# Transposes on two row halves of TensorE, and one tile for four, in a fused decoder layer

## The chip, the cores and the metric

One core of a Trainium2 chip runs the whole kernel. The metric is the device time of one execution in microseconds, the median over several runs. TensorE (PE) multiplies, ScalarE (ACT) copies and casts and evaluates functions, VectorE (DVE) does elementwise work, GpSimd (POOL) small elementwise work and some DMA issues, SyncE (SP) issues most DMAs. Each engine takes its instructions in the order of its own queue and waits by semaphores for the others.

## The reference

```python
# x (1, 512, 1024) float32, D_FF = 2816
x = x + 0.5 * rms_norm(swiglu_ffn(rms_norm(x, g0), ffn1_w_in, ffn1_w_out), p0)
x = x + rms_norm(token_mixer(rms_norm(x, g1), w_mix_in, ..., w_mix_out), p1)
x = x + 0.5 * rms_norm(swiglu_ffn(rms_norm(x, g2), ffn2_w_in, ffn2_w_out), p2)

def swiglu_ffn(x, w_in, w_out):
    gate, up = split(x @ w_in, 2)
    return (silu(gate) * up) @ w_out
# token_mixer: h @ w_in, then 4 heads of a gated linear recurrence (HGRN2) and 4 heads of a
# stabilised mLSTM, each normalised and gated, side by side (y, 512 x 1024), then y @ w_mix_out
```

## The kernel before, in words

The 512 tokens are four token tiles of 128 (i = 0 to 3). Every float32 product is made of three matmuls of a high and a low part: `mm3` (L198 to L200, and the like at L549, L560, L619, L1004, L1012) multiplies high by high, high by low and low by high. The high part of an operand is a cast by ACT, the low part is what DVE gets when it subtracts the high part from the operand.

Products contract over the model dimension, so activations are transposed first. A transpose of a 128x128 block is a matmul with the block as stationary operand and the identity as moving operand; it lands in PSUM. `turn` (L364) puts four of them, the four k-tiles of one half h of the 1024 columns of a token tile, into one PSUM bank, and then ACT casts the bank of 512 columns into the high part in `xq` and DVE subtracts into the low part. Where the place is: `to_t` and `two` (L370, L371) at the boundary of FFN 1 and mixer and for y, `part` (L384, L386, and a plain copy to `xf` at L388) at the heads of the two FFNs for the token tiles 0 and 1. For tiles 2 and 3 `sums` makes combinations out of the same kind of transposes, because the FFNs' first products are done with a Strassen-like scheme over sums of halves (`xf` holds what the sums need).

`xq` is four SBUF tiles, one for each half of the tokens and half h of the model dimension; each holds the high and the low part (b) of four k-tiles of 256 tokens. Tile 0 has 16 columns more for each part, which `xh[0]` uses at the FFNs' heads:

```python
xq = {n: self.cp.tile([P, 2 * D + 2 * STEP * (n == 0)], F32R, name=f"xq{n}") for n in (1, 2, 3, 0)}
```

Other transposes: `ek` (L1403, two groups of six, copied to `kdt`), `qk` (L1672, six, whose results DVE multiplies into `kw`); the latter follow directly on L1632, matmuls of the mLSTM's scores which already run on the two row halves of the array.

The order of the work is that in which the program issues it; a scheduler of the framework places instructions in each engine's queue by priority and by what they read and write, and it sets the waits between the engines by the address ranges of the accesses to a tile. Weights are cast and subtracted beside the products (L294 and L296; with a row factor L299 and L302) into a pool `w`.

The places in order of time: boundary of FFN 1 and mixer (331 to 349 us), `ek` (405 and 449), `qk` (485), the first half of y (536, into `mix_out0`), the second half of y (549 to 559), the head of FFN 2 (579 and 582), where the residual stream and the normed input (`xn` or `hf`, L481) of each token tile are made one after the other: ACT squares and sums (L453), POOL takes the power (L458), DVE multiplies (L481), PE transposes, ACT casts, DVE subtracts.

Of the kernel before, what the change touches and what calls it, by code (L numbers as in the profile page):

```python
# [8 lines left out]
F32 = mybir.dt.float32  # L9
# [5 lines left out]
P = 128  # L15
# [108 lines left out]
class Layer:  # L124
    def __init__(self, ctx, tc, aps):
        self.tc, self.nc = tc, tc.nc
        self.__dict__.update(aps)
        nc = self.nc
        pool = lambda name, **kw: ctx.enter_context(tc.tile_pool(name=name, bufs=1, **kw))
        self.cp, self.wp, self.sp, self.psp = pool("cp"), pool("wp"), pool("sp"), pool("psp", space=PSUM)  # L130
        self.uid, self.hold = 0, ()
        self.wt, self.free, self.slot = None, deque(), {}

        self.ident = self.cp.tile([P, P], F32, name="ident")
        make_identity(nc, self.ident)
        self.nhalf = self.cp.tile([P, 8], F32, name="nhalf")
        nc.gpsimd.memset(self.nhalf, -0.5)
        self.xs = self.cp.tile([P, NT, D], F32, name="xs")

        xq = {n: self.cp.tile([P, 2 * D + 2 * STEP * (n == 0)], F32R, name=f"xq{n}") for n in (1, 2, 3, 0)}  # L140
        self.xt = [xq[n] for n in range(4)]
        self.xq = [t[:, : 2 * D].rearrange("p (b k t) -> p b k t", b=2, k=KH) for t in self.xt]

        x0 = self.xt[0].rearrange("p (b x) -> p b x", b=2)[:, :, :D].rearrange("p b (k t) -> p b k t", k=KH)
        self.xh = [x0, *self.xq[1:]]
        self.prm = self.cp.tile([P, 36], F32, name="prm")
        self.dram = dram = ctx.enter_context(tc.tile_pool(name="sums", bufs=1, space=bass.MemoryType.DRAM))
        self.sums_of = {
            (f, h, k2): dram.tile([P, 4, QUARTER], F32, name=f"{f}sums{h}_{k2}")
            for f in ("f1", "f2") for h in range(2) for k2 in OUT[f][h] if k2 in QUARTERED[f][h]  # L150
        }
# [212 lines left out]
            self.nc.tensor.transpose(pt[:, c * P : (c + 1) * P], src[:, k * P : (k + 1) * P], self.ident)  # L364
        return pt.rearrange("p (c t) -> p c t", c=4)

    def two(self, dst, i, src):

        v = slice((i % 2) * P, (i % 2 + 1) * P)
        self.nc.scalar.copy(dst[:, 0, :, v], src)  # L370
        self.low = self.nc.vector.tensor_tensor(dst[:, 1, :, v], src, dst[:, 0, :, v].bitcast(F32), op=ALU.subtract)  # L371

    def to_t(self, i, src, halves=(0, 1)):

        for h in halves:
            self.two(self.xq[2 * (i // 2) + h], i, self.turn(src, h))

    def part(self, i, h, src):

        pv = self.turn(src, h)  # L380
        v = slice(i * P, (i + 1) * P)
        dst = self.xh[h][:, :, :, v]
        yield
        self.nc.scalar.copy(dst[:, 0], pv)  # L384
        yield
        self.nc.vector.tensor_tensor(dst[:, 1], pv, dst[:, 0].bitcast(F32), op=ALU.subtract)  # L386
        yield
        self.nc.scalar.copy(self.xf[h][:, :, v], pv)  # L388
        yield

    def sums(self, i, src):
# [37 lines left out]
    def to_s(self, i, src):  # L429

        if i < 2:
            for h in range(2):
                g = self.part(i, h, src)
                for _ in range(3):
                    next(g)
                self.copies.append(g)
        else:
            self.gs.append(self.sums(i, src))
            next(self.gs[-1])
# [955 lines left out]
    def hgrn_edges(self, p, d):  # L1395

        nc = self.nc
        qd = self.qd[:, 2 * p : 2 * p + 2, :]
        nc.vector.tensor_tensor(qd, self.q[p][:, :, P:], qd, op=ALU.mult)
        for a in range(2):  # L1400
            pt = self.ps()
            for c in range(NT - 1):
                nc.tensor.transpose(pt[:, c * P : (c + 1) * P], d[:, a, c * P : (c + 1) * P], self.ident)  # L1403
            nc.scalar.copy(self.kdt[:, 2 * p + a, :], pt[:, : 3 * P])

    def hgrn_level(self, p, n, ke):

# [229 lines left out]
    def mlstm_scores(self, mc):  # L1637

        nc = self.nc
        self.mend = mc.tile([P, NH, NT], F32, name="mend")  # L1640
        self.pT = mc.tile([P, NH, T], F32, name="pT")
        w = mc.tile([P, NT, NH], F32, name="w")
        self.qdm = mc.tile([P, 2, 3 * P], F32, name="qdm")
        H = [self.mlstm_head(h) for h in range(NH)]

        next(H[0])
        next(H[1])
        for h in range(0, NH, 2):
# [20 lines left out]
        turned = [self.ps() for _ in range(2)]  # L1669
        for p, pt in enumerate(turned):  # L1670
            for c in range(3):
                nc.tensor.transpose(pt[:, c * P : (c + 1) * P], self.qk[:, 2 + p, c * P : (c + 1) * P], self.ident)  # L1672
        for p in range(2):
            wp = self.col(8)[:, :6]
            nc.vector.tensor_copy(wp.rearrange("p (c a) -> p c a", a=2), w[:, :3, 2 * p : 2 * p + 2])
            nc.vector.tensor_tensor(
                self.kw[:, p].rearrange("p c (a d) -> p (c a) d", a=2),
                turned[p][:, : 3 * P].rearrange("p (n d) -> p n d", d=64),
                wp[:, :, None].broadcast_to([P, 6, 64]),
                op=ALU.mult,  # L1680
            )
# [96 lines left out]
    def mixer(self):  # L1778
# [3 lines left out]
        with tc.tile_pool(name="ma", bufs=1) as ma:  # L1782
# [35 lines left out]
            with tc.tile_pool(name="mc", bufs=1) as mc:  # L1818
# [8 lines left out]
                self.until("hg")  # L1827
                self.chunks(self.hgrn_values, FILL[3])
                self.until("mo")
                for i in range(NT):  # L1830
                    self.to_t(i, self.y[:, i], (0,))
                self.mix_out0()

    def values_mv(self, ma, i, ps):
# [12 lines left out]
    def mix_out0(self):  # L1847
# [130 lines left out]
```

## Time and profile before

| | |
|---|---|
| median of 3 runs | 916.1 us (916.0 to 916.24) |
| the profiled execution | 916.13 us, span 914.4 us, mean granted clock 0.999 |
| PE busy | 906.1 us, 99% of the span, 7330 instructions |
| DVE, ACT, POOL busy | 84%, 57%, 20% |
| costliest groups on PE | L619 237.4 + 178.0 us, L1012 80.9, L1004 79.2 |
| transposes of L364 | 128 in all, 0.14 us for a weight load's record, 0.27 for a matmul's |

Records of matmuls overlap: an instruction's duration on PE holds the time until its result is out, and the next one starts while it runs. The rate is read from the distance between starts, or from a merged row's length less that of one, over their number less one.

### The profile page before, as it was taken

To read this page: it belongs to the slowest core of one execution; us is meant where nothing else is said; L and a number is where in the kernel's file an instruction comes from. 1 tells how busy PE (TensorE), PEld (TensorE's weight loads), DVE (VectorE), ACT (ScalarE), POOL (GpSimd) and SP (SyncE) were. 2 spreads that over 40 slices of the span, in tenths; PEclk is the share of its full clock that TensorE was granted. 3 is DMA by queue.
4 is the path that set the end of the run, shared out by engine and by line. 5 is a ranking of instruction groups with operands and counts; after the bars stand their busy time and mean duration, and the time that the engine had idled before them with its cause. 6 is when DMAs were issued, how large, how long until landed. Compare 5 with 4: busy or idle time off the path is not lost.

```text
span 914.4 us, 18150 instructions
## 1 busy us (share of the span) xinstructions
PE 906.1 (99%) x7330; PEld 874.9 (96%) x7330; DVE 767.2 (84%) x1005; ACT 522.0 (57%) x749; POOL 183.7 (20%) x256
## 2 busy tenths in 40 slices
PE   9999999999999999999999999999999999999997
PEld 8999999999999999998888887899999999999997
DVE  6899988889888876799896556799999889998886
ACT  7645545557566567957643345684454545757661
POOL 2541112121111047742230300322000000010002
PEclk9999999999999999999999999999999999999999
DMA  9355779775897815898953126253344445378542
GB/s 306 88 165 136 189 188 216 187 159 138 219 280 233 258 55 144 162 192 207 214 112 109 47 70 213 65 161 102 97 148 139 138 123 159 104 231 246 170 146 93
DMA packets 127921, 146.51 MB, mean 160 GB/s; under 512 B 16335, under 2 KB 100303, under 8 KB 127837
## 3 DMA queue, kind: packets, MB, share of 16 engines
q1 hardware_dynamic: 111868, 130.14, 46.4%
q0 software_dynamic: 15680, 14.69, 11.9%
q8 instruction: 57, 0.93, 0.4%
q10 hardware_dynamic: 288, 0.52, 0.2%
q14 instruction: 28, 0.22, 0.1%
HBM read 143.20 MB, written 31.48 MB: 191 GB/s over the span
## 4 chain that ended last, share of the span: by engine, by line
PE 62%; ACT 0%; DVE 0%; DVEq 0%; POOLq 0%; issue 0%; POOL 0%; ACTq 0%
PE ps L619 23%; PE ps L1012 8%; PE ps L549 6%; PE ps L198 5%; PE ps L200 5%; PE ps L199 5%; PE ps L1004 4%; PE ps L560 1%; PE ps L1441 1%; PE ps L364 1%; PE ps L1540 0%; PE ps L1742 0%; PE ps L1491 0%; PE ps L1715 0%; PE ps L1739 0%; PE ps L1717 0%
## 5 line engine op out<-in xcount | busy, mean ns | idle before, releaser
L294 ACT CAST w<-raw 128x1024 fp32r<-128x1024 f32 x246 | 250.6, 1027 | 192.0 <-PE ps L619 91.1
L296 DVE TENSOR_TENSOR w<-raw,w 128x1024 fp32r<-128x1024 f32 x246 | 299.4, 1221 | 30.3 <-ACT w L294 28.9
L619 PE MATMUL ps<-xq,w 128*128 128x256 f32 x2016 | 237.4, 277 | 0.0
L619 PEld LDWEIGHTS ps<-xq,w 128*128 128x128 f32 x2016 | 233.3, 188 | 0.1
L619 PE MATMUL ps<-sq,w 128*128 128x256 f32 x1512 | 178.0, 276 | 0.0
L619 PEld LDWEIGHTS ps<-sq,w 128*128 128x128 f32 x1512 | 174.6, 188 | 0.0
L310 DVE TENSOR_TENSOR raw<-raw,raw 128x1024 f32<-128x1024 f32 x72 | 89.7, 1252 | 7.5 <-DMA raw<-in_ffn_w_in_dram 6.2
L1012 PE MATMUL ps<-w,hs 128*128 128x256 f32 x672 | 80.9, 276 | 0.0
L1004 PE MATMUL ps<-w,hs 128*128 128x256 f32 x672 | 79.2, 276 | 0.0
L1012 PEld LDWEIGHTS ps<-w,hs 128*128 128x128 f32 x672 | 78.3, 188 | 0.0
L1004 PEld LDWEIGHTS ps<-w,hs 128*128 128x128 f32 x672 | 77.5, 188 | 0.0
L198 PE MATMUL ps<-w,xq 128*128 128x512 f32 x176 | 71.1, 405 | 0.1
L199 PE MATMUL ps<-w,xq 128*128 128x512 f32 x176 | 68.6, 391 | 0.0
L200 PE MATMUL ps<-w,xq 128*128 128x512 f32 x176 | 68.6, 391 | 0.0
L549 PE MATMUL ps<-xq,w 128*128 128x256 f32 x480 | 55.7, 277 | 0.0
L944 POOL DMA_DIRECT2D f2sums<-in_ffn_w_out_dram x15 | 20.0, 1507 | 177.5 <-DMA f2sums<-in_ffn_w_out_dram 177.0
L549 PEld LDWEIGHTS ps<-xq,w 128*128 128x128 f32 x480 | 54.9, 188 | 0.5 <-issue 0.5
L884 ACT CAST hs<-hf 128x1024 fp32r<-128x1024 f32 x32 | 33.7, 1054 | 28.0 <-PE ps L1012 20.3
L885 DVE TENSOR_TENSOR hs<-hf,hs 128x1024 fp32r<-128x1024 f32 x32 | 39.1, 1223 | 9.0 <-ACT hs L884 8.4
L944 POOL DMA_DIRECT2D f1sums<-f1sums x26 | 22.3, 859 | 110.1 <-DMA f1sums<-in_ffn_w_out_dram 56.1
L944 POOL DMA_DIRECT2D f2sums<-f2sums x30 | 26.3, 905 | 87.1 <-DMA f2sums<-in_ffn_w_out_dram 42.4
L310 POOL TENSOR_TENSOR raw<-raw,raw 128x1024 f32<-128x1024 f32 x12 | 32.6, 2724 | 40.9 <-DVE w L296 40.7
(263 smaller groups left out, 1232.9 us busy)
## 6 DMA issues: line engine op xcount, KB each, us to landing
raw<-in_ffn_w_in_dram SPq DMA_DIRECT2D x98, 512.0 KB, 4.7
raw<-in_ffn_w_out_dram SPq DMA_DIRECT2D x44, 512.0 KB, 5.1
raw<-in_w_mix_in_dram SPq DMA_DIRECT2D x28, 512.0 KB, 5.7
raw<-f2sums SPq DMA_DIRECT2D x15, 512.0 KB, 5.2
raw<-f1sums SPq DMA_DIRECT2D x13, 512.0 KB, 7.0
raw<-in_w_mix_out_dram SPq DMA_DIRECT2D x8, 512.0 KB, 4.3
f2sums<-in_ffn_w_out_dram SPq DMA_DIRECT2D x30, 128.0 KB, 5.0
f2sums<-in_ffn_w_out_dram SPq DMA_DIRECT2D x15, 256.0 KB, 6.1
```

Source lines behind the costliest of these rows:

```text
L198: mm(ps, sh, mh, start=start, stop=False, **kw)
L199: mm(ps, sh, ml, start=False, stop=False, **kw)
L200: mm(ps, sl, mh, start=False, stop=stop, **kw)
L294: nc.scalar.copy(hi, raw)
L296: self.low = nc.vector.tensor_tensor(lo, raw, hi.bitcast(F32), op=ALU.subtract)
L310: added = (nc.vector if late else nc.gpsimd).tensor_tensor(o, o, c, op=ALU.add)
L549: mm(ps[:, u0:u1], w[:, a, k, :], self.xop(k, b, u0, u1), start=k + n + m == 0, stop=k == ND - 1 and n == 2, skip_group_check=True,)
L619: self.nc.tensor.matmul(ps[:, c], wb[b][:, k, v], left[d][:, k, :], start=first and a + n + k == 0, stop=n == 2 and k == KH - 1, skip_grou ...
L885: self.nc.vector.tensor_tensor(lo, src, hi.bitcast(F32), op=ALU.subtract)
L944: nc.gpsimd.dma_start(to[:, a:b], v, accum_op=ALU.add)
L1004: mm(out, a[kk][:, i * P : (i + 1) * P], w[:, b, kk, QUARTER * v : QUARTER * (v + 1)], start=begin and c == kk == n == 0, stop=kk == 1 and ...
L1012: mm(ps[:, QUARTER * c : QUARTER * (c + 1)], A[a][:, c], B[b], start=begin and c == n == 0, stop=n == 2, skip_group_check=True,)
```

## The change

98 transposes are done as two transposes of 64 rows each, on the two row halves of the array. `turns` takes a list of up to eight blocks; for each it issues one transpose of the tokens 0 to 63 into the first of two PSUM banks, and one of the tokens 64 to 127 into the second. A bank so holds one half of the tokens of a tile (or of two tiles, `to_t2`) for eight blocks, 512 columns. A cast or a subtraction takes one bank, as before, but its result now goes to both halves h (or both token tiles), by an access pattern made with `pair`. The four `xq` tiles become one, since such a pattern must lie in one tile. The second half of y is transposed two token tiles at a time. The 32 transposes at the start of FFN 1 and the 16 in `sums` of FFN 2 stay as they are.

```diff
-        xq = {n: self.cp.tile([P, 2 * D + 2 * STEP * (n == 0)], F32R, name=f"xq{n}") for n in (1, 2, 3, 0)}
-        self.xt = [xq[n] for n in range(4)]
+        xq = self.cp.tile([P, 8 * D + 2 * STEP], F32R, name="xq")
+        self.xt = [xq[:, 2 * D * o : 2 * D * (o + 1) + 2 * STEP * (o == 3)] for o in (3, 0, 1, 2)]
...
+    def turns(self, srcs):
+        pts = [self.ps() for _ in range(2)]
+        for n, src in enumerate(srcs):
+            for u, pt in enumerate(pts):
+                r = slice(64 * u, 64 * u + 64)
+                self.nc.tensor.transpose(pt[:, 64 * n : 64 * n + 64], src[r], self.ident[r, r])
+        return [pt[:, : 64 * len(srcs)] for pt in pts]
...
+    def pair(self, a, b):
+        return bass.AP(a.tensor, a.offset, [a.ap[0], [b.offset - a.offset, 2], *a.ap[1:]])
...
+    def to_t(self, i, src):
+        x = self.xq[2 * (i // 2) : 2 * (i // 2) + 2]
+        for u, pt in enumerate(self.turns(self.tiles(src, ND))):
+            hi, lo = (self.pair(*(t[:, b, :, self.at(i, u)] for t in x)) for b in range(2))
+            self.parts(hi, lo, pt.rearrange("p (h k t) -> p h k t", h=2, t=64))
...
+    def part2(self, i, u, pt):
+        pv = pt.rearrange("p (h k t) -> p h k t", h=2, t=64)
+        v = self.at(i, u)
+        hi, lo = (self.pair(*(self.xh[h][:, b, :, v] for h in range(2))) for b in range(2))
+        self.nc.scalar.copy(hi, pv)
+        self.nc.vector.tensor_tensor(lo, pv, hi.bitcast(F32), op=ALU.subtract)
+        yield
+        self.nc.scalar.copy(self.pair(*(x[:, :, v] for x in self.xf)), pv)
         yield
...
         if i < 2:
-            for h in range(2):
-                g = self.part(i, h, src)
-                for _ in range(3):
-                    next(g)
+            for u, pt in enumerate(self.turns(self.tiles(src, ND))):
+                g = self.part2(i, u, pt)
+                next(g)
                 self.copies.append(g)
...
-                for i in range(NT):
-                    self.to_t(i, self.y[:, i], (0,))
+                for i in (0, 2):
+                    self.to_t2(i, 0, [self.y[:, i + n, :W] for n in range(2)])
...
-                if part:
-                    self.to_t(i, self.y[:, i], (1,))
+                if part and i % 2 == 0:
+                    self.to_t2(i, 1, [self.y[:, i + n, W:] for n in range(2)])
```

The places of `ek` and `qk` are changed in the same way (two calls of `turns` with six blocks each, and one with six). Lines move down: L364 splits into L364 (`turn`) and L373 (`turns`), L370 and L371 become L384 and L385, L384 and L386 of `part` become L423 and L424 of `part2`, L453 L490, L481 L518, L619 L656.

How it moves instructions: three places. The rows below are the engines' queues, in order; `xq_78`, `xq_75` and so on are the four tiles, `ps_...` PSUM banks, and the brackets name the engines that a row waits for.

ACT's queue at the head of FFN 2, where `xn` of tile 0 and `hf` of tile 1 have been transposed, before:

```order
443 L384 CAST xq_78<-ps_6607 128x4x128 [waits PE_49]
444 L384 CAST xq_75<-ps_6614 128x4x128 [waits PE_49]
445 L453 ACTIVATE junk_6594,col_6592<-xs 128x512 [waits DVE_49,Activation_49]
446 L453 ACTIVATE junk_6599,col_6597<-xs 128x512 [waits DVE_49,Activation_49,Pool_49]
447 L384 CAST xq_78<-ps_6633 128x4x128 [waits PE_49]
448 L384 CAST xq_75<-ps_6640 128x4x128 [waits PE_49]
449 L453 ACTIVATE junk_6661,col_6659<-ps_6434 128x512 [waits PE_49,Activation_49,Pool_49]
```

and after:

```order
443 L423 CAST xq<-ps_6686 128x2x4x64 [waits PE_49]
444 L490 ACTIVATE junk_6673,col_6671<-xs 128x512 [waits DVE_49,Activation_49]
445 L490 ACTIVATE junk_6678,col_6676<-xs 128x512 [waits DVE_49,Activation_49,Pool_49]
446 L423 CAST xq<-ps_6687 128x2x4x64 [waits DVE_49,PE_49]
447 L423 CAST xq<-ps_6720 128x2x4x64 [waits DVE_49,PE_49]
448 L423 CAST xq<-ps_6721 128x2x4x64 [waits DVE_49,PE_49]
449 L490 ACTIVATE junk_6756,col_6754<-ps_6513 128x512 [waits PE_49,Activation_49,Pool_49]
```

One cast moves behind the two squares, and three of the four casts wait for DVE besides PE.

DVE's queue at the same place, before:

```order
635 L386 TENSOR_TENSOR xq_78<-ps_6607,xq_78 128x4x128 [waits Activation_49]
636 L386 TENSOR_TENSOR xq_75<-ps_6614,xq_75 128x4x128 [waits Activation_49]
637 L481 SCALAR_TENSOR_TENSOR xn_6604<-xs,col_6602,gpre_6493 128x512 [waits DVE_49,Pool_49]
638 L481 SCALAR_TENSOR_TENSOR xn_6604<-xs,col_6602,gpre_6493 128x512 [waits DVE_49]
639 L386 TENSOR_TENSOR xq_78<-ps_6633,xq_78 128x4x128 [waits Activation_49]
640 L386 TENSOR_TENSOR xq_75<-ps_6640,xq_75 128x4x128 [waits Activation_49]
```

and after:

```order
635 L424 TENSOR_TENSOR xq<-ps_6686,xq 128x2x4x64 [waits Activation_49]
636 L518 SCALAR_TENSOR_TENSOR xn_6683<-xs,col_6681,gpre_6572 128x512 [waits DVE_49,PE_49,Pool_49]
637 L518 SCALAR_TENSOR_TENSOR xn_6683<-xs,col_6681,gpre_6572 128x512 [waits DVE_49]
638 L424 TENSOR_TENSOR xq<-ps_6687,xq 128x2x4x64 [waits Activation_49]
639 L424 TENSOR_TENSOR xq<-ps_6720,xq 128x2x4x64 [waits Activation_49]
640 L424 TENSOR_TENSOR xq<-ps_6721,xq 128x2x4x64 [waits Activation_49]
```

The second subtraction for tile 0 moves behind the two products that make `xn` of tile 2.

ACT's queue at the first half of y, where `mo` is the gate of the mLSTM's output and `w` a weight of `mix_out0`, before:

```order
411 L299 ACTIVATE w<-raw_6087,prm 128x512 [waits DMAHW7_49,PE_49]
412 L1843 ACTIVATE mo_6217<-ps_6007 128x512 [waits PE_49,Pool_49]
413 L370 CAST xq_78<-ps_6220 128x4x128 [waits PE_49]
414 L370 CAST xq_78<-ps_6227 128x4x128 [waits PE_49]
415 L370 CAST xq_76<-ps_6234 128x4x128 [waits PE_49]
416 L370 CAST xq_76<-ps_6241 128x4x128 [waits PE_49]
417 L299 ACTIVATE w<-raw_6087,prm 128x512
```

and after:

```order
411 L299 ACTIVATE w<-raw_6134,prm 128x512 [waits DMAHW7_49,PE_49]
412 L1877 ACTIVATE mo_6264<-ps_6054 128x512 [waits PE_49,Pool_49]
413 L299 ACTIVATE w<-raw_6134,prm 128x512
414 L384 CAST xq<-ps_6267 128x2x4x64 [waits PE_49]
415 L384 CAST xq<-ps_6268 128x2x4x64 [waits PE_49]
416 L384 CAST xq<-ps_6289 128x2x4x64 [waits PE_49]
417 L384 CAST xq<-ps_6290 128x2x4x64 [waits PE_49]
```

The second half of that weight moves ahead of the casts; the first two casts hold the tokens of tiles 0 and 1 together, the next two those of tiles 2 and 3.

More of the change, by code (lines that the diff above doesn't have):

```diff
@@ L365, in turn, with tiles, parts, at @@
         return pt.rearrange("p (c t) -> p c t", c=4)
[L367 to L376, printed above, removed]
+    def turns(self, srcs):
[5 more added lines that the diff above has]
+        return [pt[:, : 64 * len(srcs)] for pt in pts]
+    def tiles(self, src, n=4):
+        return [src[:, k * P : (k + 1) * P] for k in range(n)]
+    def pair(self, a, b):
+        return bass.AP(a.tensor, a.offset, [a.ap[0], [b.offset - a.offset, 2], *a.ap[1:]])
+    def parts(self, hi, lo, src):
+        self.nc.scalar.copy(hi, src)
+        self.low = self.nc.vector.tensor_tensor(lo, src, hi.bitcast(F32), op=ALU.subtract)
+    def at(self, i, u):
+        return slice((i % 2) * P + 64 * u, (i % 2) * P + 64 * u + 64)
+    def to_t(self, i, src):
[3 more added lines that the diff above has]
+            self.parts(hi, lo, pt.rearrange("p (h k t) -> p h k t", h=2, t=64))
+    def to_t2(self, i, h, srcs):
+        x = self.xq[2 * (i // 2) + h]
+        for u, pt in enumerate(self.turns([t for src in srcs for t in self.tiles(src)])):
+            hi, lo = (self.pair(*(x[:, b, :, self.at(c, u)] for c in range(2))) for b in range(2))
+            self.parts(hi, lo, pt.rearrange("p (c k t) -> p c k t", c=2, t=64))
     def part(self, i, h, src):
@@ L388, in part @@
         self.nc.scalar.copy(self.xf[h][:, :, v], pv)
+        yield
[5 more added lines that the diff above has]
+        self.nc.vector.tensor_tensor(lo, pv, hi.bitcast(F32), op=ALU.subtract)
+        yield
+        self.nc.scalar.copy(self.pair(*(x[:, :, v] for x in self.xf)), pv)
         yield
@@ L1399, in hgrn_edges @@
         nc.vector.tensor_tensor(qd, self.q[p][:, :, P:], qd, op=ALU.mult)
[L1400 to L1404, printed above, removed]
+        for u, pt in enumerate(self.turns([t for a in range(2) for t in self.tiles(d[:, a], NT - 1)])):
+            kd = self.kdt[:, 2 * p : 2 * p + 2, :].rearrange("p a (c k) -> p a c k", c=3)[:, :, :, 64 * u : 64 * u + 64]
+            nc.scalar.copy(kd, pt.rearrange("p (a c k) -> p a c k", a=2, c=3))
     def hgrn_level(self, p, n, ke):
@@ L1668, in mlstm_scores @@
         nc.scalar.activation(self.qdm, self.qdm, AF.Exp)
[L1669 to L1673, printed above, removed]
+        for a, pt in enumerate(self.turns([t for p in range(2) for t in self.tiles(self.qk[:, 2 + p], 3)])):
             wp = self.col(8)[:, :6]
-            nc.vector.tensor_copy(wp.rearrange("p (c a) -> p c a", a=2), w[:, :3, 2 * p : 2 * p + 2])
+            p = a
+            nc.vector.tensor_copy(
+                wp.rearrange("p (n c) -> p n c", c=3), w[:, :3].rearrange("p c (n a) -> p n c a", a=2)[:, :, :, a]
+            )
             nc.vector.tensor_tensor(
-                self.kw[:, p].rearrange("p c (a d) -> p (c a) d", a=2),
-                turned[p][:, : 3 * P].rearrange("p (n d) -> p n d", d=64),
+                self.kw.rearrange("p n c d -> p (n c) d")[:, :, 64 * a : 64 * a + 64],
+                pt.rearrange("p (n d) -> p n d", d=64),
                 wp[:, :, None].broadcast_to([P, 6, 64]),
```

## The prediction

> **What bounds the kernel now.** I read the busy shares first, then PE's waits, then PE's timeline at each place where a changed transpose stands, and last ACT and DVE at the same places.
>
> ```profile
> PE 906.1 (99%) x7330; PEld 874.9 (96%) x7330; DVE 767.2 (84%) x1005; ACT 522.0 (57%) x749; POOL 183.7 (20%) x256
> PEclk9999999999999999999999999999999999999999
> ```
> ```profile
> PE ps L619 <- ACT xq L384: 0.2, 1, 0.2
> ```
>
> PE is busy for 906.1 of 914.4 us at full clock, and apart from the start the only wait that the list of PE's waits holds is 0.2 us. So a nanosecond saved on PE counts, as long as what follows in PE's queue is ready, and a wait that reaches PE counts in full. The profiled execution took 916.13 us (span 914.4, 1.7 around it); the median of the runs is 916.1, so sums against it stand against the median too.
>
> **Prices on PE.** The old transpose, the row-half matmuls that the kernel already has (L1632), and the weight loads:
>
> ```profile
> 477.88 0.39 PE L200 MATMUL ps<-w,xq 128*128 128x512 f32 x1
> 478.20 1.16 PE L1632 MATMUL ps<-qk 64*128 64x128 f32 x16
> 479.29 0.50 PE L198 MATMUL ps<-w,xq 128*128 128x512 f32 x1
> 479.63 0.39 PE L199 MATMUL ps<-w,xq 128*128 128x512 f32 x1
> 479.86 0.40 PE L200 MATMUL ps<-w,xq 128*128 128x512 f32 x1
> ```
> ```profile
> 535.89 1.91 PE L364 MATMUL ps<-ident,y 128*128 128x128 f32 x16
> 537.56 0.48 PE L198 MATMUL ps<-w,xq 128*128 128x512 f32 x1
> 537.87 0.40 PE L199 MATMUL ps<-w,xq 128*128 128x512 f32 x1
> 538.18 0.50 PE L200 MATMUL ps<-w,xq 128*128 128x512 f32 x1
> 538.52 0.40 PE L198 MATMUL ps<-w,xq 128*128 128x512 f32 x1
> ```
> ```profile
> 478.19 0.97 PEld L1632 LDWEIGHTS ps<-qk 64*128 64x128 f32 x16 [0.35 <-DVE e L1622]
> ```
> ```profile
> L364 PEld LDWEIGHTS ps<-ident,y x32: 138/140/142, 535.7 to 558.8; 128*128 128x128 f32 x32
> L364 PE MATMUL ps<-ident,y x32: 270/273/273, 535.9 to 558.9; 128*128 128x128 f32 x32
> ```
> ```profile
> 7.98 0.20 PEld L364 LDWEIGHTS ps<-ident,xn 128*128 128x128 f32 x2 [0.45 <-DVE xn L754]
> ```
>
> Sixteen transposes span 1.91 us and one lasts 0.273, so they follow each other every (1.91 - 0.27)/15 = 0.109 us; a 512-column matmul passes every 0.23 (479.63 to 479.86). Where nothing moved through the array yet (7.98), two transposing weight loads stood (0.20 - 0.14) = 0.06 us apart. A half transpose moves 64 columns instead of 128, so the moving part falls to 0.055, and the load at 0.06 is then the longer: I take 0.058 for a pair, if the halves run side by side. That they can is seen at L1632: eight pairs' weight loads take (0.97 - 0.19)/7 = 0.111 us per pair, about what one 128-column matmul takes alone. The bounds of a pair: 0.055 below (moving alone), 0.111 above (L1632's own, with twice the columns).
>
> Changing to row halves and back: from L200 at 477.88 to L199 at 479.63 are 1.75 us; two 512-column matmuls and eight pairs are 0.46 + 0.89, so the switches cost 0.40. The new groups have half as long a first weight load to wait for (0.06 against 0.11): 0.35, which I use.
>
> So a group of n pairs in a place of its own costs 0.35 + 0.058n against 0.109n: eight pairs -0.06, six pairs +0.05, sixteen -0.47. Gross, 98 x 0.051 = 5.0 us come off and 10 x 0.35 = 3.5 go back on: PE alone would gain 1.5. What follows is where that goes.
>
> **Boundary of FFN 1 and mixer (four groups of eight).**
>
> ```profile
> 337.86 0.84 PE L1004 MATMUL ps<-w,hs 128*128 128x256 f32 x6
> 338.79 5.73 PE L560 MATMUL ps<-xq,w 128*128 128x256 f32 x48
> ```
> ```profile
> 337.67 1.07 ACT L294 CAST w<-raw 128x1024 fp32r<-128x1024 f32 x1
> ```
>
> Before L560 PE stands still about 0.25 (six at 0.113 end at 338.54) for the cast of w that ends at 338.74. What the first two groups gain or lose disappears there: 0. The last two: -0.12. ACT and DVE do as many casts and subtractions as before, each of 512 columns as before, though in eight pieces of 64 instead of four of 128; no row here shows pieces of 64, so I keep their durations, and a few per cent more on them would matter in the ladder below alone.
>
> **ek (two groups of six): +0.10.** **qk (six):**
>
> ```profile
> 483.60 1.16 PE L1632 MATMUL ps<-qk 64*128 64x128 f32 x16
> 484.69 0.87 PE L1672 MATMUL ps<-ident,qk 128*128 128x128 f32 x6
> ```
>
> These stand right behind a block of row-half matmuls, so no switch is added: -6 x 0.051, with a little for the end, -0.28. The products kw on DVE are as many and as large. On SP and POOL the order stays, but for one small DMA of maxima that moves up by a place; no wait of PE names it: 0.
>
> **First half of y (sixteen).** PE would be done 0.47 sooner, but now the first L198 needs two casts, since a cast holds 64 tokens of two token tiles, and the queue of ACT has one more half of w (L299) ahead of them:
>
> ```profile
> 536.15 0.60 ACT L1843 ACTIVATE mo<-ps 128x512 f32<-128x512 f32 x1
> 536.65 2.05 ACT L370 CAST xq<-ps 128x512 fp32r<-128x512 f32 x4
> 538.54 0.77 ACT L299 ACTIVATE w<-raw,prm 128x512 fp32r<-128x512 f32 x1
> ```
>
> mo ends its slot at 536.65; L299 takes 0.65 to 537.3, two casts at 0.51 end at 538.3, and PE starts L198 at about 538.5 instead of 537.64. Of that 0.86, 0.28 come back, because the stalls between 537.56 and 538.52 (0.31 + 0.31 + 0.34 instead of 3 x 0.23) go: the low halves come later in PE's new order. The fourth cast adds 0.1: +0.7. Bounds: -0.47 if the cast is in time, +1.2 if the low halves stall it as well.
>
> **Second half of y (eleven, one and four, now sixteen at once).**
>
> ```profile
> 546.90 2.77 ACT L299 ACTIVATE w<-raw,prm 128x512 fp32r<-128x512 f32 x4 [7.59 <-PE ps L200]
> 549.57 1.05 ACT L370 CAST xq<-ps 128x512 fp32r<-128x512 f32 x2
> ```
> ```profile
> L198 PEld LDWEIGHTS ps<-w,xq 128*128 128x128 f32 x176 | 33.1, 188 | 7.5 <-ACT xq L370 0.7 <-issue 0.6
> ```
>
> Before: 16 x 0.109 and 0.7 of waits for the casts (the last row) make 2.4. After: 0.35 + 0.93, then the wait for the second cast, which ends at 550.6 on an ACT that is busy until 549.57: 0.8 to 0.9. Together 2.15: -0.3.
>
> **Head of FFN 2 (two groups of eight).** Here the change adds waits.
>
> ```profile
> 583.28 1.05 ACT L384 CAST xq<-ps 128x512 fp32r<-128x512 f32 x2
> 586.04 0.60 ACT L453 ACTIVATE junk<-ps 128x512 f32<-128x512 f32 x1 [1.71 <-PE ps L200]
> ```
> ```profile
> 582.34 1.27 DVE L386 TENSOR_TENSOR xq<-ps,xq 128x512 fp32r<-128x512 f32 x2
> 584.47 1.41 DVE L481 SCALAR_TENSOR_TENSOR xn<-xs,col,gpre 128x512 f32<-128x512 f32 x2 [0.86 <-POOL col L458]
> 585.80 1.28 DVE L386 TENSOR_TENSOR xq<-ps,xq 128x512 fp32r<-128x512 f32 x2
> ```
> ```profile
> 582.13 1.03 PE L364 MATMUL ps<-ident,hf 128*128 128x128 f32 x8
> 585.76 2.99 PE L619 MATMUL ps<-xq,sq 128*128 128x256 f32 x24
> ```
> ```profile
> 583.89 0.55 POOL L458 TENSOR_TENSOR col<-col,nhalf 128x1 f32<-128x1 f32 x1
> ```
>
> Before, the last two casts were done at 584.3, well ahead of L619 at 585.76; DVE subtracted behind them at leisure. After, three of the four casts wait for DVE as well as for PE, because the writes over two regions of the one xq tile are taken to overlap: cast and subtraction become a ladder. And DVE's queue has the two products xn of the next token tile between the first and the second subtraction. xn waits for POOL's power, which ends at 584.44, whatever the transposes do. So: xn 584.47 to 585.80, subtraction to 586.45, third cast 586.55 to 587.07, subtraction to 587.8, fourth cast 587.9 to 588.4, and the first L656 (the old L619), which reads all 256 tokens, starts at about 588.5 instead of 585.76: +2.75. The steps use 0.52 for a cast (half of 1.05), 0.65 for a subtraction (half of 1.28), and 0.1 to hand over. The chain hangs on the norm of the mixer's output, not on the transposes, so the 0.12 that the two groups would gain is lost in the wait. Behind PE on this wait are all of FFN 2's products; its sums for the third tile slip with it by 2.2 us, less than PE does, and ask for nothing sooner. After the head the list of waits has nothing to take the delay up. Bounds: 0 if the waits on DVE refer to older subtractions, +3.1 if handing over takes 0.2 each time.
>
> **The sum.** 0 - 0.12 + 0.10 - 0.28 + 0.7 - 0.3 + 2.75 = +2.85: 916.1 + 2.8 = 918.9 us.
>
> **Rivals.** (1) The head's ladder does not bind: the order names the engine waited for, not which of its instructions, and if the older subtraction is meant, the casts run at 583.3 as before. Against it: DVE's own queue holds xn between, and the third subtraction cannot pass it. Then the sum is 0, or 916.1, within 0.2%. (2) Faster: ladder absent and the casts for y in time, so that PE's own 1.5 remains, and at 0.055 a pair 1.8: 914.4. Decided by whether L198's cast ends by 537.0; ACT's queue speaks against it. (3) The pairs cost 0.111, as L1632's do, so nothing comes off and the switches stay: the last two boundary groups +0.75, the first two +0.5 after the stall, ek +0.75, qk 0, y +0.8 and +0.2, head +2.75: +5.75, or 921.9. For it speaks L1632's load spacing; against it the 0.06 at 7.98, which is a transposing load, as the new ones are.
>
> [...]
>
> **Chances.** My forecast 0.60 (918.0 to 919.8 alone); rival 3, 0.14; rival 1, 0.18, nearly all within 0.2%; rival 2, 0.08. A measurement of this kernel tells about 0.2%, 1.8 us, from no change. So slower 0.74, same 0.18, faster 0.08. The range reaches from 915.3, inside rival 1, to 922.0, above rival 3.
>
> **What would show it.** Right: PE idle just before the first L656 of FFN 2 for about 2.7 us, put down to ACT's cast L423; casts and subtractions there taking turns; transposes L373 in pairs 0.06 apart; 0.1 more between the groups and their neighbours. Wrong: L656 starting at 585 to 586, pairs 0.11 apart, or L198 behind the first half of y starting before 538.

## The result, and the profile after

| | before | after |
|---|---|---|
| median, us | 916.05 (915.46 to 916.24, 4 runs) | 921.55 (920.99 to 923.13, 4 runs) |
| ratio | 1 | 1.0064, 95% interval 1.0046 to 1.0081 |
| profiled execution, us | 916.13 | 923.13 |
| PE busy, us | 906.1 (99%) | 907.4 (98%) |
| mean granted clock | 0.999 | 0.995 |

The change costs about 5.5 us. It is slower, as forecast, inside the range (915.3 to 922.0), but almost twice the +2.8 of the point forecast. The profiled execution after is the slowest of its four; it shows where the time goes, but its sum is 1.6 us above the median.

The list of PE's waits after (total, times, longest, us). Before, it had three rows: 1.2 and 0.3 at the start, and L619 for a cast, 0.2.

```profile
PE ps L656 <- ACT xq L423: 3.0, 1, 3.0
PE ps L198 <- ACT xq L384: 1.8, 2, 1.2
PE ps L194 <- POOL ones L172: 1.2, 1, 1.2
PE ps L656 <- DVE ps L675: 0.8, 1, 0.8
PE ps L597 <- ACT w L294: 0.3, 1, 0.3
PE ps L656 <- ACT xq L411: 0.2, 1, 0.2
PE ps L364 <- DVE xn L791: 0.2, 1, 0.2
```

The first row is the stall at the head of FFN 2. The second is two waits for casts of y. The fourth, some 80 us behind the first, was not forecast.

PE's timeline at the head, after (start, length, engine, line, names; what it waited for in brackets):

```profile
585.55 0.39 PE L200 MATMUL ps<-w,xq 128*128 128x512 f32 x1
588.98 5.49 PE L656 MATMUL ps<-xq,sq 128*128 128x256 f32 x24 [3.04 <-ACT xq L423]
594.26 1.48 PE L364 MATMUL ps<-ident,xn 128*128 128x128 f32 x8
595.51 0.72 PE L656 MATMUL ps<-xq,sq 128*128 128x256 f32 x4
```

and rows of before that answer to the end of this stretch, and to the place just ahead of the head:

```profile
588.58 1.03 PE L364 MATMUL ps<-ident,xn 128*128 128x128 f32 x8
589.37 0.84 PE L619 MATMUL ps<-xq,sq 128*128 128x256 f32 x5
...
579.31 0.48 PE L198 MATMUL ps<-w,xq 128*128 128x512 f32 x1
```

L656 starts at 588.98 where L619 started at 585.76: 3.2 us lost. But its 24 matmuls then take 5.28 us to the next row (588.98 to 594.26), and before they took 2.82 (585.76 to 588.58). The clock says why. Stretches after, with the granted clock third from the end:

```profile
586.00:588.00 2.00, 0.00 (x0) 0.00 (x0) 1.27 (x2) 0.59 (x1) 0.00 (x0) 1.00 0.00 0
588.00:589.00 1.00, 0.02 (x1) 0.02 (x1) 0.04 (x1) 0.66 (x2) 0.00 (x0) 0.67 0.03 8
589.00:595.00 6.00, 6.00 (x28) 6.00 (x29) 4.63 (x7) 4.98 (x12) 2.56 (x5) 0.50 0.09 20
595.00:596.00 1.00, 1.00 (x10) 1.00 (x9) 0.75 (x2) 1.00 (x2) 0.18 (x1) 0.91 1.06 372
```

A mean of 0.67 over 588 to 589 is half clock for 0.66 us, so the clock fell at 588.34, 2.6 us after PE's last matmul had passed (585.55 + 0.23) and 2.4 us after the end of its record (585.55 + 0.39), and came back at 595.2. The page's row of clocks in 40 slices hardly shows it: one 8 among nines.

The ladder itself, ACT and then DVE, after:

```profile
586.66 0.59 ACT L423 CAST xq<-ps 128x512 fp32r<-128x512 f32 x1 [2.73 <-DVE xq L424]
588.34 0.59 ACT L423 CAST xq<-ps 128x512 fp32r<-128x512 f32 x1 [1.09 <-DVE xq L424]
```
```profile
584.56 1.41 DVE L518 SCALAR_TENSOR_TENSOR xn<-xs,col,gpre 128x512 f32<-128x512 f32 x2 [1.47 <-POOL col L495]
585.89 0.69 DVE L424 TENSOR_TENSOR xq<-ps,xq 128x512 fp32r<-128x512 f32 x1
587.28 0.69 DVE L424 TENSOR_TENSOR xq<-ps,xq 128x512 fp32r<-128x512 f32 x1 [0.71 <-ACT xq L423]
588.96 0.69 DVE L424 TENSOR_TENSOR xq<-ps,xq 128x512 fp32r<-128x512 f32 x1 [0.99 <-ACT xq L423]
```

xn, subtraction, cast, subtraction, cast, then L656: each starts within 0.1 us of the end of the one before it, except the last cast, which comes 0.37 behind its subtraction.

The pairs, and the stall at the first half of y:

```profile
578.35 0.39 PE L200 MATMUL ps<-w,xq 128*128 128x512 f32 x1
578.67 0.72 PE L373 MATMUL ps<-ident,xn 64*128 64x64 f32 x16
579.32 0.50 PE L198 MATMUL ps<-w,xq 128*128 128x512 f32 x1
579.65 0.40 PE L199 MATMUL ps<-w,xq 128*128 128x512 f32 x1
```
```profile
535.80 1.21 PE L373 MATMUL ps<-ident,y 64*128 64x64 f32 x32
538.19 0.50 PE L198 MATMUL ps<-w,xq 128*128 128x512 f32 x1 [1.18 <-ACT xq L384]
```

Sixteen pairs in 1.21 us, one matmul being 0.22: 0.062 us a pair. From 578.35 to 579.65 are 1.30 us; less 0.46 for two long matmuls and 0.50 for eight pairs, the switches cost 0.34. And 579.32 against 579.31 before: the two profiles stand level where the head begins. But the last six matmuls ahead of the first changed transposes start at 330.11 after and at 330.54 before, so the changed kernel was 0.43 ahead before anything of the change had run, and what comes ahead of the head costs about 0.43 in this profile. In the profiles of experiments one, three, four, eight and eleven, which have the same order there, it costs 0.10 to 0.21.

### The profile page after: what moved, and what is told of

Its sections match the earlier page's. It is cut to its first block, busy times and chain, and to the rows that moved or that the text cites. A ratio compares the mean times of both kernels' runs of the same rounds, so it can differ in the third digit from the quotient of the medians.

```text
span 921.4 us, 18348 instructions
## 1 busy us (share of the span) xinstructions
PE 907.4 (98%) x7428; PEld 874.5 (95%) x7428; DVE 768.4 (83%) x1005; ACT 522.4 (57%) x749; POOL 184.3 (20%) x256
## 4 chain that ended last, share of the span: by engine, by line
PE 58%; DVE 2%; ACT 1%; issue 1%; DMA 1%; POOL 0%; DVEq 0%; POOLq 0%; ACTq 0%
PE ps L656 21%; PE ps L1049 8%; PE ps L586 6%; PE ps L198 5%; PE ps L200 5%; PE ps L199 5%; PE ps L1041 4%; PE ps L597 1%; PE ps L1476 1%; DMA raw<-in_ffn_w_in_dram 1%; DVE raw L310 1%; DVE w L296 1%; PE ps L1575 0%; PE ps L1776 0%; PE ps L1526 0%
## 5 line engine op out<-in xcount | busy, mean ns | idle before, releaser
L656 PE MATMUL ps<-xq,w 128*128 128x256 f32 x2016 | 237.1, 277 | 0.0
L656 PEld LDWEIGHTS ps<-xq,w 128*128 128x128 f32 x2016 | 233.1, 188 | 0.0
L656 PE MATMUL ps<-sq,w 128*128 128x256 f32 x1512 | 178.1, 276 | 0.8 <-DVE ps L675 0.8
L656 PEld LDWEIGHTS ps<-sq,w 128*128 128x128 f32 x1512 | 174.6, 188 | 1.0 <-DVE ps L675 1.0
L198 PE MATMUL ps<-w,xq 128*128 128x512 f32 x176 | 71.2, 405 | 1.8 <-ACT xq L384 1.8
L200 PE MATMUL ps<-w,xq 128*128 128x512 f32 x176 | 68.2, 391 | 0.0
L198 PEld LDWEIGHTS ps<-w,xq 128*128 128x128 f32 x176 | 33.1, 188 | 9.5 <-ACT xq L384 2.3
```

The costliest lines, as they stand in the source:

```text
L198: mm(ps, sh, mh, start=start, stop=False, **kw)
L200: mm(ps, sl, mh, start=False, stop=stop, **kw)
L656: self.nc.tensor.matmul(ps[:, c], wb[b][:, k, v], left[d][:, k, :], start=first and a + n + k == 0, stop=n == 2 and k == KH - 1, skip_grou ...
```

## The experiments

**One: the head of FFN 2 as before, the rest of the change kept.**

```diff
-            for u, pt in enumerate(self.turns(self.tiles(src, ND))):
-                g = self.part2(i, u, pt)
-                next(g)
+            for h in range(2):
+                g = self.part(i, h, src)
+                for _ in range(3):
+                    next(g)
```

> The changed kernel, except that the two groups of transposes at the head of FFN 2 go back to whole 128x128 transposes and their casts by halves of the model dimension (`part` as before); everything else of the change stays, the single xq tile too. Theory A (the ladder of casts and subtractions at the head is the loss, 3.2 us of idle PE and about 2.6 us at half clock behind it): L656 starts right behind the last L200, the clock stays at 1.00, and the time is 916.0 to 916.3, as the profile after stands level with the one before (0.00 us) where the head begins. Rival B (the loss lies in the transposes themselves, their switches or the single tile): the time stays above 919.

Measured: 915.81 us (915.24 to 916.84, 11 runs), ratio to before 1.0005 (0.9997 to 1.0014). L657, the same product, starts behind the last L200 again:

```profile
585.30 0.39 PE L200 MATMUL ps<-w,xq 128*128 128x512 f32 x1
585.52 3.02 PE L657 MATMUL ps<-xq,sq 128*128 128x256 f32 x24
```

So the whole loss hangs on the head; the other 82 transposes in row halves, and the single tile, come to nothing that can be measured. Rival B falls.

**Two: the waits taken away by the layout, the row halves kept.**

```diff
-        self.xh = [x0, *self.xq[1:]]
+        self.xh = list(self.xq)
```

> The changed kernel with one line different: the view xh[0] of the FFNs' heads loses its 16-column gap between high and low part, so that the pair patterns of the high and of the low parts have the same stride. The transposes stay in row halves everywhere. In the queues the three waits of casts on DVE are gone and both subtractions of tile 0 stand ahead of xn again. Theory A (the waits come from patterns of unequal stride that are taken to overlap, and they alone make the stall): 915.8 to 916.2, a hundredth of a per cent or so below e1_head_old because the head's two groups gain 0.06 us each. Rival C (casts and subtractions in pieces of 64 from row-half transposes are too late for L656 in any case): PE idle before L656 for over 1 us, 917.5 or more.

Measured: two groups. Six executions at 914.85 to 915.85 us, and six at 921.8 to 926.6 (median of all 918.84, ratio 1.0050, 1.0017 to 1.0083, which says little here). The profile belongs to the second group, at 921.83, and yet its head is free of the stall:

```profile
585.33 0.39 PE L200 MATMUL ps<-w,xq 128*128 128x512 f32 x1
585.55 1.11 PE L656 MATMUL ps<-xq,sq 128*128 128x256 f32 x8
587.00 2.10 PE L656 MATMUL ps<-xq,sq 128*128 128x256 f32 x16 [0.34 <-DVE xq L424]
```

L656 starts right behind the last L200. So the waits on DVE made the stall, and row halves as such are in time but for 0.34 us (rival C falls). What makes six executions longer is something else. In this profile the matmuls of 256 columns follow each other more slowly from about 740 us on:

```profile
680.00:720.00 40.00, 40.00 (x355) 40.00 (x354) 36.98 (x39) 20.84 (x25) 0.00 (x0) 1.00 0.42 130
760.00:800.00 40.00, 40.00 (x342) 40.00 (x341) 37.89 (x47) 25.79 (x36) 0.00 (x0) 1.00 0.38 118
```

355 matmuls in 40 us, then 342, at a granted clock of 1.00 in both. The kernel before passes 355 in the second stretch.

**Three, four and eight: PE kept busy in the stall.** Matmuls of the identity by itself ahead of the first L656 of FFN 2, 26 (shown), 12 and 6 of them; the results are not used.

```diff
             self.lag()
+            if n == 0:
+                ps = self.bank[p, t] = self.ps()
+                for _ in range(26):
+                    self.nc.tensor.matmul(ps[:, :P], self.ident, self.ident, start=True, stop=True)
             self.prod(p, t, False)
```

> The changed kernel with 26 more matmuls of the identity by itself (128 columns, about 0.107 us each, 2.8 us in all) on PE just before the first L656 of FFN 2, into the bank that L656 then starts anew; nothing reads their results. They fill most of the 3.0 us in which PE stands still there. Theory D (the half clock behind the stall comes from PE having been idle): the granted clock behind L656 stays 1.00 and the time falls by about 2.6 us to 918.7 to 919.3, although PE has more to do. Rival E (the clock falls for another reason, as the row-half mode or the load of the other engines): half clock as before, 921.5.

> The same with 12 such matmuls, so that PE is idle for about 1.7 us only. Theory D, if the clock needs more than about 2 us of idleness to fall: 918.9 as e3_fill26. If less than 1.7 us will do: 921.5. The stall of 1.18 us at the first half of y left the clock at 1.00.

> The changed kernel with 6 matmuls of the identity ahead of the first L656 of FFN 2. Each took about 0.23 us in e4_fill12 (2.84 us for 12), twice what I had taken, so 12 left PE idle for only 0.35 us with the clock at 1.00, and 6 leave about 1.8 us. Theory D with a limit between 1.2 us (the stall at y, clock 1.00) and 2.5 us (clock down 2.5 us into the stall of the changed kernel): if the limit is above 1.8, clock 1.00 and the level of e4_fill12, 920.2; if below, a half clock of some us as in the changed kernel and 921.5 to 922.

Measured: 26 gave 921.86 us (ratio 1.0071, 1.0058 to 1.0084), 12 gave 920.16 (1.0053, 1.0040 to 1.0066), 6 gave 919.65 (1.0043, 1.0030 to 1.0056). The expectation of the first was off, because each of these matmuls is two records and takes 0.22 us, twice the 0.109 at which whole transposes follow each other, so 26 filled the stall twice over: L656 started at 592.57, but at full clock, and its 24 matmuls took 2.90 us. With 6:

```profile
585.79 1.50 PE L753 MATMUL ps<-ident 128*128 128x128 f32 x12
588.99 3.04 PE L656 MATMUL ps<-xq,sq 128*128 128x256 f32 x24 [1.70 <-ACT xq L423]
591.88 1.03 PE L364 MATMUL ps<-ident,xn 128*128 128x128 f32 x8
```
```profile
588.00:590.00 2.00, 1.01 (x8) 1.01 (x9) 1.03 (x2) 1.65 (x4) 0.28 (x2) 1.00 0.01 4
590.00:592.00 2.00, 2.00 (x20) 2.00 (x19) 1.70 (x4) 1.06 (x3) 0.54 (x1) 1.00 0.00 0
```

L656 starts at 588.99, as without them (588.98), and runs in 2.89 us instead of 5.28, at a clock of 1.00. PE with more work is done sooner: theory D holds. In time the six matmuls bring 1.3 to 1.9 us (919.65 against 920.97 and 921.55), less than the 2.9 that the profile after shows for the half clock; the intervals of the ratios overlap, so that size is known to about 1 us. For the same reason 12 and 6 stay above the 918.7 to 919.3 that was hoped for: in most executions the half clock costs less than in the profiled one (see eleven). Counted from the end of the last record, 1.70 us of idleness here left the clock at 1.00, and 2.40 us in the profile after lowered it.

**Five and six: the first half of y in whole transposes as well.** Five on top of one, six on top of two.

```diff
-                for i in (0, 2):
-                    self.to_t2(i, 0, [self.y[:, i + n, :W] for n in range(2)])
+                for i in range(NT):
+                    x, v = self.xq[2 * (i // 2)], slice((i % 2) * P, (i % 2 + 1) * P)
+                    self.parts(x[:, 0, :, v], x[:, 1, :, v], self.turn(self.y[:, i], 0))
```

> As e1_head_old, and the first half of y goes back to whole transposes, a cast for each token tile (the second half of y, ek, qk and the boundary stay in row halves, the single xq tile stays). In ACT's queue the four casts stand ahead of the second half of w again. Theory A: the 0.84 us that PE lost there (from -0.21 to +0.63 us against the profile before) come back, 0.7 to 0.8 us below e1_head_old: 915.0, 0.1% faster than before. Rival B: the wait of 1.2 us for a cast there only moves to the second half of y: level with e1_head_old.

> As e2_no_gap (the head in row halves, no gap, so no waits on DVE) with the first half of y as in e5. Theory A: as e5, less the 0.12 of the head's two groups: 914.9 in the executions that do not show the 4% longer pitch of PE that the second half of e2_no_gap's profile shows (6 of its 12 executions were at 921.8 and above, the others at 914.9 to 915.9). If that pitch goes with the missing gap, it is seen here again; if it was a passing state of the chip, it is not.

Measured: five 916.18 us (915.2 to 917.3, ratio 1.0003, 0.9995 to 1.0012), level with one (1.0005). In the list of PE's waits the two waits for the casts of y, 1.8 us, become one of 0.7 (the second half of y), but the time does not show it, and expectation A is missed; a wait of 0.3 for DVE some 75 us behind the head stands in both. What became of the rest is below what these runs can tell. Six again fell into two groups, six executions at 914.61 to 915.28 and six at 924.4 to 926.4: the longer executions go with the missing gap.

**Seven: the kernel before, without the gap.** The one line of experiment two, in the kernel before.

> The kernel before with the same one line: no 16-column gap in xh[0]; the queues are the same word for word. Theory A: 916, no change, since the gap only matters to the pair patterns. Rival F (the missing gap itself slows PE in some executions): a part of the executions at 921 and above, as in e2_no_gap.

Measured: 926.92 us (926.79 to 939.24, 5 runs), ratio 1.0122 (1.0107 to 1.0137). Same instructions in the same order, no added wait, and in the profile fewer matmuls pass at the same clock. (The profiled execution is the slowest of the five, 939.24 us, so its rows show more than the median has.) The stretch 100 to 200 us before, and in this kernel:

```profile
100.00:200.00 100.00, 100.00 (x882) 100.00 (x882) 85.00 (x86) 52.55 (x65) 20.65 (x22) 1.00 0.83 195
```
```profile
100.00:200.00 100.00, 100.00 (x851) 100.00 (x850) 80.06 (x80) 50.00 (x61) 20.70 (x22) 1.00 0.79 187
```

Rival F holds, and more so than it was put: all five executions are longer. The 16 columns, which matter to no result, are worth about 11 us.

**Nine and ten: a gap on both halves.** xq is 32 columns longer, xh[0] and xh[1] have the same strides, so no cast waits for DVE; nine keeps row halves everywhere, ten has the first half of y in whole transposes.

```diff
-        xq = self.cp.tile([P, 8 * D + 2 * STEP], F32R, name="xq")
-        self.xt = [xq[:, 2 * D * o : 2 * D * (o + 1) + 2 * STEP * (o == 3)] for o in (3, 0, 1, 2)]
+        xq = self.cp.tile([P, 8 * D + 4 * STEP], F32R, name="xq")
+        at = (6 * D + 2 * STEP, 0, 2 * D + 2 * STEP, 4 * D + 2 * STEP)
+        self.xt = [xq[:, o : o + 2 * D + 2 * STEP * (n < 2)] for n, o in enumerate(at)]
...
-        self.xh = [x0, *self.xq[1:]]
+        xh = [
+            t.rearrange("p (b x) -> p b x", b=2)[:, :, :D].rearrange("p b (k t) -> p b k t", k=KH) for t in self.xt[:2]
+        ]
+        self.xh = [*xh, *self.xq[2:]]
```

> The whole change with row halves everywhere, and both xh[0] and xh[1] with the 16-column gap (xq is 32 columns longer), so that the pair patterns have equal strides and no cast waits for DVE; the queues are those of e2_no_gap word for word, only addresses differ. Theory G (the 4% longer pitch came from the missing gap, not from the order or the row halves): no execution above 918, and 915.3 to 915.8, like the undisturbed half of e2_no_gap. If the longer pitch shows again, it belongs to something else, or to any addresses but the tuned ones.

> The same, with the first half of y in whole transposes as in e5. Theory A: 0.3 to 0.6 us below e9, 914.9 to 915.3, which is 0.04 to 0.1% faster than the kernel before: the best version that these experiments point to. If it is level with e9, the cast that PE waited for at the first half of y only moves on.

Measured: 920.88 us (ratio 1.0061, 1.0048 to 1.0073) and 920.65 (1.0052, 1.0040 to 1.0065). The stall at the head is gone in both, as meant, but the pitch is longer in places (nine, 350 to 380 us: 255 matmuls, before 267, at a clock of 1.00), and that eats the gain. Theory G is missed as it was put: it is not the gap alone, other addresses do it as well.

**Eleven: the changed kernel again.**

> The changed kernel again, unchanged, for a second profile. Theory A and D: 3.0 us of idle PE before L656 of FFN 2 again, and a stretch at half clock behind it of 4 to 7 us, which may be longer or shorter than the 6.5 us of the first profile (its four executions lay between 920.99 and 923.13).

Measured: 920.97 us (ratio 1.0053, 1.0038 to 1.0069). The second profile, the last L200, L656 and the clock:

```profile
586.83 0.39 PE L200 MATMUL ps<-w,xq 128*128 128x512 f32 x1
590.26 5.49 PE L656 MATMUL ps<-xq,sq 128*128 128x256 f32 x24 [3.04 <-ACT xq L423]
```
```profile
589.00:590.00 1.00, 0.00 (x0) 0.00 (x0) 0.26 (x1) 0.38 (x1) 0.00 (x0) 0.82 0.00 0
590.00:596.00 6.00, 5.74 (x27) 5.74 (x28) 4.37 (x6) 4.97 (x12) 2.57 (x5) 0.50 0.07 14
596.00:597.00 1.00, 1.00 (x9) 1.00 (x7) 0.88 (x2) 1.00 (x3) 0.00 (x0) 0.76 0.97 314
```

The clock falls at 589.64, 2.6 us after PE stood still, and is back at 596.48: 6.8 us at half, as in the first profile (588.34 to 595.18). The wait for DVE behind the head that cost 0.8 there is not among this profile's. Instead this execution is 1.28 us later where the head begins (585.55 there for the last L200), and that comes from ahead of the change: in 40 to 80 us 346 matmuls pass, in the first profile 355, at a clock of 1.00.

That the two profiles agree on 2.6 us looks like chance, for in these runs the clock does not follow the idle time directly. In the profiles before and after it changes in steps of 3.41 us: the half clock after is two steps long (588.35 to 595.17; 6.8 us in the second profile too), the full clock ahead of it, from 4.67 us on, 583.68 us or 171 steps, and in the kernel before the full clock lasts from 4.97 to 912.91, 266 steps. Here the clock goes with how long PE stood still within the step that has just ended. Four steps (PE's busy time first): the one that ends in the stall after; the same in experiment eight; and the ends of experiments five and ten, where PE runs out of work:

```profile
584.93:588.35 3.42, 1.01 (x5) 0.51 (x3) 2.34 (x4) 0.59 (x2) 0.00 (x0) 1.00 0.00 0
585.21:588.62 3.41, 2.08 (x16) 1.77 (x14) 2.07 (x4) 0.85 (x2) 0.00 (x0) 1.00 0.00 0
906.72:910.13 3.41, 1.48 (x14) 1.28 (x12) 2.35 (x6) 0.95 (x4) 1.90 (x4) 1.00 0.68 252
911.94:915.35 3.41, 1.43 (x13) 1.23 (x11) 2.35 (x6) 0.95 (x4) 1.86 (x4) 1.00 0.68 252
```

PE is idle for 2.41, 1.33, 1.93 and 1.98 us of them; half clock follows the first and the fourth (mean granted clocks of these executions 0.995, 0.999, 0.999 and 0.998). In each of the profiles before and after, the only other step at full clock with more than 1.34 us of idleness is the last one, behind PE's last matmul, with all 3.41 us idle (909.50 to 912.91 before, 916.03 to 919.44 after), and half clock follows it; it follows none of the rest. In the two profiles of the changed kernel the clock came back behind a step without idleness, and not behind the one before it, of which PE was idle for 0.63 and 0.62 us. The steps begin at another time in each execution (the full clock starts at 4.97 us before and at 4.67 after), so the same stall may bring two steps at half clock, or fewer. The mean granted clocks say so too: 0.995 and 0.994 in the two profiled executions, 0.996 to 0.998 in the other six of the changed kernel, 0.998 to 1.000 in every execution of the other versions. At 0.997 against 0.998 to 0.999, an estimate from these figures is 0.9 to 1.8 us lost to the clock, about what the six matmuls bring.

**Twelve: no waits, and no address moved.** The cast keeps its pair, the low parts are subtracted in two pieces without one; the first half of y is as in five.

```diff
-        hi, lo = (self.pair(*(self.xh[h][:, b, :, v] for h in range(2))) for b in range(2))
-        self.nc.scalar.copy(hi, pv)
-        self.nc.vector.tensor_tensor(lo, pv, hi.bitcast(F32), op=ALU.subtract)
+        self.nc.scalar.copy(self.pair(*(self.xh[h][:, 0, :, v] for h in range(2))), pv)
+        for h in range(2):
+            hi, lo = (self.xh[h][:, b, :, v] for b in range(2))
+            self.nc.vector.tensor_tensor(lo, pv[:, h], hi.bitcast(F32), op=ALU.subtract)
```

> The changed kernel with every address as it is (gap and all), row halves everywhere but in the first half of y (whole transposes there, as in e5), and the low parts at the head of FFN 2 subtracted in two pieces of 256 columns, one for each half of the model dimension, without a pair pattern; the cast keeps its pair. No cast waits for DVE any more, with four more small instructions on DVE. Theory A with G (the waits made the loss, and the longer pitch of e9 and e10 came from moved addresses): no idle PE at the head, no half clock, no execution above 918, 915.0 to 915.5, that is 0.03 to 0.08% faster than the kernel before, at the edge of what can be told. Rival: 917 or more, if the row halves at the head cost something besides the waits, or if the longer pitch comes with them and not with the addresses.

Measured: 916.66 us (915.18 to 917.79, 11 runs), ratio 1.0009 (1.0000 to 1.0018). Behind the start no stall over 0.7 us, no half clock, no execution above 918: A and G hold in that. But it is no gain; L657 now waits 0.5 us for the low parts at the head. None of the versions beats the kernel before beyond what can be told.

## Why the prediction was right, and where it was off

- **Prices on PE: right.** A pair 0.062 us for 0.058, the switches 0.34 for 0.35. The weight loads agree: the 16 of the first group at the head (578.67) span 0.58 us and one lasts 0.14, so 0.063 us a pair. Rival 3, with the 0.111 a pair of L1632, gave 921.9 and so lies nearer to the measured time than the forecast; only the rows tell that it is wrong.
- **What comes ahead of the head: right in sum, near enough.** Forecast 0 - 0.12 + 0.10 - 0.28 + 0.7 - 0.3 = +0.1; measured 0.43 in the profile after and 0.10 to 0.21 in five others. That this profile stands 0.01 us behind the one before at 579.3 is luck. Place by place, by the distance between the same products in the two profiles: boundary +0.13 (-0.17 to -0.20 in the five others), ek +0.34 where +0.10 was put, qk -0.24, first half of y +0.71, second half -0.45, and -0.06 for the first group of the head. The first L198 behind the first half of y, forecast for 538.5, started at 538.19 in an execution that was 0.2 ahead there (and the 537.64 that the forecast set against it is 537.56 in the row it shows). PE's busy time rose by 1.3 us, but 2.9 of that is the half clock told of below; without it PE has 1.6 less to do, where the forecast had 1.5. Experiment one's profile, which has no half clock, has 2.6 less (903.44 against 906.07), so that agreement is loose.
- **The ladder: right as a mechanism, short by 0.5.** L656 at 588.98 instead of 588.5. xn came 0.1 later than in the profile before, and the handing over from the third subtraction (ended 587.97) to the fourth cast (588.34) took 0.37 where I had put 0.1. Experiments one, two and twelve show that the waits on DVE are the cause. Rival 1 fell.
- **The step that failed: the sum ends with the stall, and has no price for what runs behind it.** I wrote "After the head the list of waits has nothing to take the delay up" and priced the stall at its own length. It has a second price, the clock: the profile after shows 24 matmuls in 5.28 us instead of 2.82, and the eight transposes in 1.25 instead of 0.79, 2.9 us in all. Experiments four and eight, in which the same wait stands at the same place with PE busy for part of it, show that idleness brings it. Only one place of the kernel before could have hinted at it, since PE was never idle for long between its start and its end: PE is done at 908.2 us, and the granted clock falls to 0.50 at 912.9. Taken at its word, that place, with 4.75 us from PE's end to the fall, would have let a stall of 2.75 us pass; in experiment ten 1.98 us of idleness in a step were enough. With one step of 3.41 us at half clock, as long as the steps measured after, an estimate of 1.7 us lost comes on top, and 918.9 becomes 920.6.
- **The remainder.** 3.2 + 2.9 are 6.1 us in the first profile; the wait for DVE at 668 us (0.8) makes it 6.9 of the 7.0 by which that execution (923.13) is longer than the profiled one before. The median is 5.5 above. The other executions are shorter at least in part because their half clock is (see their mean clocks under eleven): 3.2 and the estimate of 0.9 to 1.8 are 4.1 to 5.0. What makes the rest is not shown; experiments four and eight, at full clock, also stay 0.8 to 1.5 above what a stall of 3.2 explains.

## What to carry to other kernels

Patterns that reach over two regions of one tile can be taken to overlap where they do not, if their strides differ, and then an independent cast waits for a subtraction; look at the waits of each moved instruction, and at what stands in the queue of the engine waited for. Price a stall on a busy TensorE by the clock too (here half clock followed 1.98 us of idleness in a step of 3.41 us, and did not follow 1.93), expect that price to vary from one execution to the next (mean clocks of 0.994 to 0.998 in eight executions of the changed kernel), and fill the stall with idle work if it cannot be removed (six matmuls brought 1.3 to 1.9 us). Where a tile's layout carries an odd gap, measure it alone before a change touches it.

## What the runs showed of the hardware

- In the profiles before and after, the granted clock changed in steps of 3.41 us (266 at full clock before; 171, then two at half and 95 at full clock after). Of their steps at full clock, and of the three shown of experiments five, eight and ten, half clock followed those in which PE was idle for 1.98, 2.41 and, twice, 3.41 us, and none with 1.93 or less; in the two profiles of the changed kernel it came back behind a step without idleness. The stall of 3.0 us brought 6.8 us of half clock in these two profiles, and less in most of the other six executions by their mean clocks (0.996 to 0.998 against 0.995 and 0.994).
- PE's pitch of 256-column matmuls was 4% longer (342 instead of 355 in 40 us, at a granted clock of 1.00) from about 740 us on in experiment two, and in 100 to 200 us of experiment seven (851 instead of 882 matmuls). By their times it came and went between executions of one kernel, and how often went with the layout of an operand by 16 or 32 columns: all five executions of the kernel before without its gap were at 926.79 or above, six of twelve of the changed one without it at 921.8 or above, but none of the 11 executions each of experiments one, five and twelve, nor of the 61 of the kernel before beside them, with the addresses as they were. Short stretches stand there too (the kernel before, 680 to 720 us: 347 matmuls; the changed one again, 40 to 80: 346). Why is open; it was not tried which operand's address does it.
- Two row halves of a transpose ran side by side at the price of about one half: 0.062 us a pair after against 0.109 for a whole one before. But going to row halves and back cost 0.34 (578.35 to 579.65 after), so eight pairs in a place of their own gain 0.03 us (0.84 against 0.87).
